# Instance normalisation over 512 images: row statistics by one reduce and one Square in place of sixteen BN_STATS, with fixed engine order and whole tiles at the end

## The chip, the cores and the metric

One core of one Trainium2 chip. The metric is the device time of one execution in microseconds (us); where several runs exist the median is quoted. Before: 1258.53 us (13 runs, 1258.19 to 1258.94).

A ratio between two kernels is the mean time of one kernel's fast runs over that of the other's of the same rounds. So it isn't quite the ratio of the medians quoted here. Now and then a single run came out too long, of the kernel before as well (1264.60 and 1267.03 us). Such runs still count as fast runs and widen the intervals, so I compare medians and traces and give the interval beside them where it matters. What makes those runs long I don't know.

## The reference

```python
# x: float32 [8, 64, 32, 64, 64]; eps = 1e-5
mean = np.mean(x, axis=(2, 3, 4), keepdims=True)
var = np.var(x, axis=(2, 3, 4), keepdims=True)
return ((x - mean) / np.sqrt(var + eps)).astype(np.float32)
```

That is 512 independent images of 131,072 values. The kernel has to read 268.44 MB and write 268.44 MB, and does little arithmetic on them.

## The kernel before

Eight images make a tile of 128 partitions x 8192 values (4 MiB), 16 partitions for one image. There are 64 tiles and six buffers. A tile is loaded, its statistics are taken, a matmul with a block-diagonal matrix of ones adds up the 16 partitions of each image, a chain of five tiny operations makes a scale and a bias of the sums, and one ScalarE pass normalises the tile in place, after which it is stored.

```python
for g in range(n_groups):                       # 64 tiles
    tail = g >= n_groups - 2
    lsplit = 4 if tail else LOAD_SPLIT          # LOAD_SPLIT = NSPLIT = 1
    nsplit = 4 if tail else NSPLIT
    x_tile = xpool.tile([P, F], FP32)           # six buffers, F = 8192
    ...
    for j in range(lsplit):                     # load, by columns
        nc.sync.dma_start(out=xv3[:, j, :], in_=xg3[:, j, :])

    stats6 = spool.tile([P, NCHUNK, 6], FP32)
    for c in range(NCHUNK):                     # 16 pieces of 512
        nc.vector.bn_stats(out=stats6[:, c, :], in_=xv[:, c, :])
    mv = spool.tile([P, 2], FP32)
    nc.vector.bn_aggr(out=mv[:], in_=stats6[:])
    # ... one tiny VectorE op, the matmul into psum_t, then ACT, DVE, ACT, DVE, DVE
    #     on one column each, giving sb = (scale, bias) ...
    for h in range(nsplit):
        nc.scalar.activation(out=yv[:, h, :], in_=yv[:, h, :], func=AF.Identity,
                             bias=sb[:, 1:2], scale=sb[:, 0:1])
        nc.gpsimd.dma_start(out=og[:, h, :], in_=yv[:, h, :])     # store
```

The order of the instructions on each engine is the scheduler's. The last two tiles ("the tail") are loaded, normalised and stored in four column pieces of 2048 values.

## Time and profile before

| | before |
|---|---|
| span in the profile | 1256.8 us |
| VectorE (DVE) busy, instructions | 55%, 1345 |
| ScalarE (ACT) busy | 39% |
| bytes, mean rate | 537.03 MB, 427 GB/s |
| instruction-fetch packets | 16 |
| last load lands, last store lands | 1232.1 us, 1253.1 us |

These lines of the page of the kernel before are its slice view (40 slices of 31.4 us; a digit is the busy share in tenths), its DMA queues (packets, MB, share of 16 engines' span) and two costly groups (busy us, mean ns | idle time of the engine before them and what ended it).

```profile
span 1256.8 us, 2298 instructions
DVE  5854645646556465464554645646556465464632
DMA  9999999999999999999999999999999999999996
GB/s 400 420 432 434 433 434 434 434 433 434 432 434 433 434 434 433 432 434 434 431 434 434 433 430 431 433 433 434 432 434 433 433 434 434 432 434 434 432 407 274
...
q1 hardware_dynamic: 10080, 268.44, 49.6%
q0 software_dynamic: 10080, 268.44, 49.6%
q14 instruction: 16, 0.13, 0.0%
...
L76 DVE BATCH_NORM_STATS2 stats<-x_tile 128x6 f32<-128x512 f32 x1024 | 614.9, 684 | 452.0 <-DMA x_tile<-in_x_dram 452.0
L128 ACT ACTIVATE x_tile<-x_tile,sb 128x8192 f32<-128x8192 f32 (+1 forms) x70 | 463.3, 6626 | 49.5 <-DVE sb L113 49.5
...
x_tile<-in_x_dram SPq DMA_DIRECT2D x62, 4096.0 KB, 48.4
out_dram<-x_tile POOLq DMA_DIRECT2D x62, 4096.0 KB, 48.6
```

The DMA row is full until the last slice; no engine row is. So in the middle of the kernel only the DMA counts. VectorE's 452 us of waiting for loads are not lost time but spare capacity. Apart from the start (400 and 420), the last two columns of the rate row (407 and 274) are the only place where the DMA falls off. The row `q14 instruction` counts the packets that fetch the engines' instructions, of all engines together.

The windows view of the same kernel cuts out that place. Its columns are the stretch in us, its length, busy us (and instructions) of PE, PEld, DVE, ACT and POOL, the granted clock, the DMA engines' mean busy share, and GB/s. A DMA packet counts in the stretch in which it starts, so a share can come out a little over 1.

```profile
1160.00:1200.00 40.00, 1.12 (x4) 1.00 (x4) 22.26 (x43) 8.14 (x5) 0.53 (x1) 1.00 1.00 431
1200.00:1214.00 14.00, 0.00 (x0) 0.00 (x0) 7.16 (x13) 7.21 (x1) 0.53 (x1) 1.00 1.00 421
1214.00:1224.00 10.00, 0.56 (x2) 0.50 (x2) 3.59 (x9) 0.47 (x2) 0.00 (x0) 1.00 0.98 421
1224.00:1232.00 8.00, 0.00 (x0) 0.00 (x0) 4.74 (x9) 3.90 (x2) 0.53 (x1) 1.00 0.17 70
1232.00:1245.00 13.00, 0.56 (x2) 0.50 (x2) 3.92 (x10) 12.19 (x9) 3.19 (x6) 1.00 0.99 403
```

From 1224 to 1232 us the DMA engines are 17% busy: most of them have nothing to do.

The DMA view of the kernel before, for 1165 to 1198 us alone, shows how the two queues share the engines while the loads of the tail are in flight (q0 is the stores, q1 the loads; packets, MB, share).

```profile
q0 software_dynamic: 368, 10.94, 76.8%
q1 hardware_dynamic: 363, 3.35, 23.9%
```

The packet counts are almost equal, the bytes are not: most load packets are 8 KB there (a quarter of a row), the stores' are 32 KB (a whole row).

One more reading comes from the trace itself. Each transfer counts sixteen completions, one from each DMA engine. This table, not part of the profile page, gives for some loads of the kernel before how long after the middle completion the last one came, and when the nearest instruction-fetch packets started.

```
load landed at     126   145 | 165   262 | 282   379 | 399   496 | 516    1158 us
last minus middle  1.3   1.3 | 2.1   1.9 | 2.8   2.5 | 3.2   3.0 | 3.8     7.3 us
fetch packet at          149.7       266.5       383.4       500.3  us
```

Each of these packets is followed by a step of 0.7 to 0.9 us, and little of it is made up before the next. Not every fetch packet is: the one at 239.8 us, for instance, left the last completion where it was (2.0 us at 223 and at 243 us).

### The profile page before, as it was taken

The numbers are of one execution on the slowest core, as the hardware profiler recorded it, in microseconds if no ns is written. First come the engines' busy times: TensorE is split into PE (matmuls) and PEld (weight loads), VectorE is DVE, ScalarE is ACT, GpSimd is POOL, SyncE is SP. The second block draws the span as 40 slices with busy tenths as digits, with TensorE's granted clock in tenths as the row PEclk, the third lists the DMA queues.
The fourth block names the chain that finished last, engine by engine and source line by source line (L and its number), as shares of the span: only waits on it lengthen the run. The fifth ranks groups of instructions, "written<-read, shape, count | busy, mean of one in ns | idle before, by whom it ended". The sixth has DMA issues, their size and how long they took to land.

```text
span 1256.8 us, 2298 instructions
## 1 busy us (share of the span) xinstructions
PE 35.9 (3%) x128; PEld 32.0 (3%) x128; DVE 695.7 (55%) x1345; ACT 495.9 (39%) x201; POOL 38.2 (3%) x76
## 2 busy tenths in 40 slices
PE   0000000000000000000000000000000000000000
PEld 0000000000000000000000000000000000000000
DVE  5854645646556465464554645646556465464632
ACT  2544243342443434424334243342443434424225
POOL 0000000000000000000000000000000000000001
DMA  9999999999999999999999999999999999999996
GB/s 400 420 432 434 433 434 434 434 433 434 432 434 433 434 434 433 432 434 434 431 434 434 433 430 431 433 433 434 432 434 433 433 434 434 432 434 434 432 407 274
DMA packets 20177, 537.03 MB, mean 427 GB/s; under 512 B 2240, under 2 KB 2240, under 8 KB 2240
## 3 DMA queue, kind: packets, MB, share of 16 engines
q1 hardware_dynamic: 10080, 268.44, 49.6%
q0 software_dynamic: 10080, 268.44, 49.6%
q14 instruction: 16, 0.13, 0.0%
q8 instruction: 1, 0.02, 0.0%
HBM read 268.44 MB, written 268.44 MB: 427 GB/s over the span
## 4 chain that ended last, share of the span: by engine, by line
issue 78%; DMA 14%; DVE 3%; POOL 2%; ACT 2%; PE 0%; POOLq 0%; ACTq 0%; SPq 0%
DMA x_tile<-in_x_dram 9%; DMA out_dram<-x_tile 6%; POOL out_dram L135 2%; DVE stats L76 2%; ACT x_tile L128 2%; DVE mv L78 0%; PE psum_t L90 0%; POOLq L135 0%; ACT tmp L104 0%; DVE mv L80 0%; POOLq L169 0%; ACT tmp L95 0%; DVE sb L112 0%; DVE sb L113 0%; DVE tmp L96 0%
## 5 line engine op out<-in xcount | busy, mean ns | idle before, releaser
L76 DVE BATCH_NORM_STATS2 stats<-x_tile 128x6 f32<-128x512 f32 x1024 | 614.9, 684 | 452.0 <-DMA x_tile<-in_x_dram 452.0
L128 ACT ACTIVATE x_tile<-x_tile,sb 128x8192 f32<-128x8192 f32 (+1 forms) x70 | 463.3, 6626 | 49.5 <-DVE sb L113 49.5
L95 ACT ACTIVATE tmp<-psum_t 128x1 f32<-128x1 f32 x64 | 11.0, 171 | 684.9 <-PE psum_t L90 684.8
L135 POOL DMA_DIRECT2D out_dram<-x_tile x70 | 37.4, 534 | 1205.7 <-ACT x_tile L128 1204.3
L90 PE MATMUL psum_t<-mv,block_ones 128*128 128x2 f32 x128 | 35.9, 350 | 1200.3 <-DVE mv L80 1200.3
L90 PEld LDWEIGHTS psum_t<-mv,block_ones 128*128 128x128 f32 x128 | 32.0, 310 | 1204.1 <-issue 1094.8
L96 DVE SCALAR_TENSOR_TENSOR tmp<-psum_t,tmp 128x1 f32<-128x1 f32 x64 | 10.1, 158 | 58.7 <-ACT tmp L95 58.7
L78 DVE BATCH_NORM_AGGREGATE mv<-stats 128x2 f32<-128x96 f32 x64 | 37.6, 588 | 2.1
L104 ACT ACTIVATE tmp<-tmp,eps_tile 128x1 f32<-128x1 f32 x64 | 18.8, 294 | 14.2 <-DVE tmp L96 14.2
L112 DVE RECIPROCAL sb<-tmp 128x1 f32<-128x1 f32 x64 | 10.5, 163 | 23.5 <-ACT tmp L104 23.5
L80 DVE SCALAR_TENSOR_TENSOR mv<-mv 128x1 f32<-128x1 f32 x64 | 14.0, 219 | 2.2
L113 DVE SCALAR_TENSOR_TENSOR sb<-psum_t,sb 128x1 f32<-128x1 f32 x64 | 10.1, 158 | 2.1
masks.py:370 ACT ACT_TABLE_LOAD x1 | 1.3, 1283 | 0.8 <-PEq L155 0.8
L104 ACT ACT_TABLE_LOAD x1 | 1.3, 1283 | 0.0
L55 DVE MEMSET eps_tile<- 128x1 f32 x1 | 0.1, 59 | 0.9 <-PEq L155 0.9
masks.py:371 POOL TENSOR_SCALAR_AFFINE_SELECT block_ones<-block_ones 128x128 f32<-128x128 f32 x1 | 0.3, 332 | 2.0 <-ACT block_ones masks.py:370 2.0
masks.py:383 POOL TENSOR_SCALAR_AFFINE_SELECT block_ones<-block_ones 128x128 f32<-128x128 f32 x1 | 0.3, 344 | 0.1
masks.py:370 ACT ACTIVATE block_ones<-block_ones 128x128 uint32<-128x128 uint32 x1 | 0.3, 309 | 0.0
L155 POOL MEMSET const-float32-0.0<- 128x1 f32 x1 | 0.1, 98 | 0.3 <-issue 0.3
L155 POOL MEMSET const-bfloat16-1.0<- 128x1 bf16 x1 | 0.1, 101 | 0.0
L155 POOL MEMSET const-uint8-127<- 128x1 uint8 x1 | 0.1, 101 | 0.0
L155 POOL MEMSET const-float32-1.0<- 128x1 f32 x1 | 0.1, 98 | 0.0
## 6 DMA issues: line engine op xcount, KB each, us to landing
x_tile<-in_x_dram SPq DMA_DIRECT2D x62, 4096.0 KB, 48.4
out_dram<-x_tile POOLq DMA_DIRECT2D x62, 4096.0 KB, 48.6
x_tile<-in_x_dram SPq DMA_DIRECT2D x8, 1024.0 KB, 56.5
out_dram<-x_tile POOLq DMA_DIRECT2D x8, 1024.0 KB, 6.0
```

The costliest lines, as they stand in the source:

```text
L76: nc.vector.bn_stats(out=stats6[:, c, :], in_=xv[:, c, :])
L78: nc.vector.bn_aggr(out=mv[:], in_=stats6[:])
L80: nc.vector.scalar_tensor_tensor(out=mv[:, 1:2], in0=mv[:, 0:1], scalar=mv[:, 0:1], in1=mv[:, 1:2], op0=ALU.mult, op1=ALU.add,)
L90: nc.tensor.matmul(psum_t[:], lhsT=block_ones[:], rhs=mv[:], start=True, stop=True)
L95: nc.scalar.activation(out=tmp[:, 0:1], in_=psum_t[:, 0:1], func=AF.Square)
L96: nc.vector.scalar_tensor_tensor(out=tmp[:, 1:2], in0=psum_t[:, 1:2], scalar=float(PPI), in1=tmp[:, 0:1], op0=ALU.mult, op1=ALU.subtract,)
L104: nc.scalar.activation(out=tmp[:, 2:3], in_=tmp[:, 1:2], func=AF.Sqrt, bias=eps_tile[:, 0:1], scale=1.0 / (PPI * PPI),)
L112: nc.vector.reciprocal(out=sb[:, 0:1], in_=tmp[:, 2:3])
L113: nc.vector.scalar_tensor_tensor(out=sb[:, 1:2], in0=psum_t[:, 0:1], scalar=-1.0 / PPI, in1=sb[:, 0:1], op0=ALU.mult, op1=ALU.mult,)
L128: nc.scalar.activation(out=yv[:, h, :], in_=yv[:, h, :], func=AF.Identity, bias=sb[:, 1:2], scale=sb[:, 0:1],)
L135: nc.gpsimd.dma_start(out=og[:, h, :], in_=yv[:, h, :],)
L155: nc = _bacc.Bacc("TRN2", target_bir_lowering=False, num_devices=1)
```

## The change

The intent: fewer and cheaper VectorE instructions for the statistics. The sum comes from one reduce over the whole row on VectorE, the sum of squares from one Square with an accumulator on ScalarE at the same time, whose element output goes to a scratch tile of 8-bit floats. The program order on these two engines is fixed, and the cut of the last two tiles is dropped.

```diff
-    for g in range(n_groups):
-        lsplit = 4 if tail else LOAD_SPLIT
-        nsplit = 4 if tail else NSPLIT
+    junk = cpool.tile([P, F], mybir.dt.float8e4)
+    with tc.manual_schedule(engines={mybir.EngineType.DVE, mybir.EngineType.Activation}):
+        for g in range(n_groups):
+            lsplit = LOAD_SPLIT
+            nsplit = NSPLIT
 ...
-        for c in range(NCHUNK):
-            nc.vector.bn_stats(out=stats6[:, c, :], in_=xv[:, c, :])
-        nc.vector.bn_aggr(out=mv[:], in_=stats6[:])
-        nc.vector.scalar_tensor_tensor(...)        # mean^2 + var
+            nc.vector.reduce_sum(out=s[:, 0:1], in_=x_tile[:], axis=AX.X)
+            nc.scalar.activation(
+                out=junk[:], in_=x_tile[:], func=AF.Square,
+                accum_out=s[:, 1:2], saturate=False,
+            )
 ...   # matmul and the small chain as before, with other constants; then normalise and store
```

## The prediction

> **What bounds it now.** The DMA engines: the slice view shows them 90% busy or more in 39 of 40 slices, at 430 to 434 GB/s; 537.03 MB at 434 GB/s is 1237 of the 1256.8 us span. VectorE is 55% busy, ScalarE 39%. A tile's cycle through the six buffers is some 116 us: load 48.4 us from issue to landing, store 48.6, and only about 20 from landing to store issue. So faster statistics in the middle shorten nothing.
>
> **Costs.** Per tile the change removes sixteen BN_STATS (9.59 us in a row), BN_AGGREGATE (0.59) and one small operation (0.22). It adds a reduce over 8192 elements on VectorE and, beside it, a Square with accumulator on ScalarE. The Trainium skill, "VectorE: DVE Perf Modes", section "The perf-mode tier table", gives tensor_reduce its slowest mode only; no trace here shows one yet. Estimate from BN_STATS (599 ns per 512): 8.6 to 8.8 us. Square: the same-size Identity took 7.21, so 7.1 to 7.4. Landing to store issue falls from 20 to 18 us. ScalarE rises to 15 us of the 19.4 us period: no bottleneck.
>
> **Where I expect a gain: two places, seen at the end.**
> 1. Of the sixteen completion counts of each load, the last comes ever later than the middle one: 1.3 us at 126 us, 7.3 at 1158. It grows in steps of about 0.75 us at 8 KB instruction-fetch packets (149.7, 266.5, 383.4, 500.3, 617.1 us...), one per six tiles, when VectorE has run some 128 instructions. (The Trainium skill, "Runtime: NRT & Kernel Launch", "Instruction fetch mechanics": a sequencer fetches its instructions by DMA.) So VectorE's fetches delay one DMA engine, and each transfer ends with its slowest. VectorE goes from 21 instructions a tile to 4, some 9 fetches become about 2, and 5 us of lag go.
> 2. The tail is cut in four: its loads travel in 8 KB packets against the stores' 32 KB and get a quarter of their rate (80 against 330 GB/s, 1164 to 1200 us). The last lands at 1232.1. Stores run dry meanwhile (ScalarE's pass over tile 61 waits 9.7 us behind a BN_STATS of the next tile), and DMA share is 0.17 in 1224 to 1232. Whole-tile loads should land by 1212, and the last store be issued near 1230, while older stores still occupy the DMA.
>
> At 1164 us the trace still has 9.9 MB of loads and 25 MB of stores to move. At 434 GB/s mixed (46 us), then 420 to 432 store-only (15 MB, 35 to 36 us), that ends at about 1245, plus 1 to 3 us of remaining lag: 1247, against 1253.1 now. The last 3.7 us of span and 1.7 to the measured time stay.
>
> **Prediction: 1252.3 us** (0.5% less), 8 in 10 between 1249 and 1256.8. Faster by over 2%: 0.01; within 2%: 0.96; slower by over 2%: 0.03.
>
> **Right if:** the DMA row stays at 9 to the last slice; fetch packets drop from 16 to 7 or fewer; the lag at 1150 us is under 3 us; VectorE under 50%, ScalarE near 75%; reduce about 8.7 us.
>
> **Wrong if:** the lag is no matter of fetches (then 1256 to 1258); the stores run dry before the last, leaving a bare 18 us chain (1258 to 1262); Square's 8-bit output or accumulator takes twice as long, so that ScalarE passes 19 us a tile (much slower); or mixed traffic slows.

## The result, and the profile after

1250.34 us (9 runs, 1250.24 to 1250.45) against 1258.53 us. The ratio is 0.9935, 95% interval 0.9925 to 0.9944: 8.2 us less, a small difference but clear of the noise, and inside the predicted range.

The same lines of the page of the kernel after (here a slice is 31.2 us):

```profile
span 1248.6 us, 1262 instructions
DVE  5554534535445354453544535435345354453541
DMA  9999999999999999999999999999999999999998
GB/s 403 420 437 437 434 429 432 436 437 431 426 437 436 436 431 427 437 435 436 431 429 436 435 435 431 429 434 437 434 429 431 436 436 434 428 433 436 437 433 345
...
q14 instruction: 8, 0.06, 0.0%
...
L77 DVE TENSOR_REDUCE s<-x_tile 128x1 f32<-128x8192 f32 x64 | 555.9, 8685 | 516.4 <-DMA x_tile<-in_x_dram 516.4
L78 ACT ACTIVATE junk<-x_tile 128x8192 fp8e4<-128x8192 f32 x64 | 449.8, 7028 | 99.3 <-DMA x_tile<-in_x_dram 99.3
...
L78 ACT ACTIVATION_READ_ACCUMULATOR junk<-x_tile 128x1 f32 x64 | 11.9, 186 | 0.0
...
x_tile<-in_x_dram SPq DMA_DIRECT2D x64, 4096.0 KB, 50.8
out_dram<-x_tile POOLq DMA_DIRECT2D x64, 4096.0 KB, 47.3
```

The middle is the same as before: the trace moves 433.2 GB/s between 600 and 1150 us in both kernels. ScalarE is now 76% busy and VectorE 47%, which changes nothing. The fetch packets fell from 16 to 8; one of the 8 started 0.1 us into the span, and in the other traces it came just before the span, so like for like it is 16 against 7. The windows view of the kernel after for the same stretches:

```profile
1200.00:1214.00 14.00, 0.56 (x2) 0.50 (x2) 3.77 (x5) 9.41 (x6) 0.53 (x1) 1.00 1.04 447
1214.00:1224.00 10.00, 0.56 (x2) 0.50 (x2) 7.59 (x4) 7.00 (x5) 0.00 (x0) 1.00 0.97 419
1224.00:1232.00 8.00, 0.00 (x0) 0.00 (x0) 0.00 (x0) 6.23 (x1) 0.53 (x1) 1.00 1.05 455
1232.00:1245.00 13.00, 0.00 (x0) 0.00 (x0) 0.00 (x0) 0.00 (x0) 0.00 (x0) 1.00 0.78 338
```

The hole at 1224 to 1232 us is gone (share 0.17 to 1.05), and the DMA works until it has nothing left (0.78 in 1232 to 1245 us, in which the engines finish). The last load lands at 1212.4 us (1232.1 before), the last store is issued at 1230.5 us and lands at 1245.1 us (1253.1 before). In the DMA view for 1165 to 1198 us of the kernel after, equal packets now carry equal bytes:

```profile
q0 software_dynamic: 248, 7.34, 51.5%
q1 hardware_dynamic: 251, 7.18, 50.4%
```

Last minus middle completion of the loads near 1155 us: 1.9 us (7.3 before).

### The profile page after: what moved, and what is told of

Read it like the earlier page. It is cut to its first block, busy times and chain, and to the rows that moved or that the text cites. A ratio compares the mean times of both kernels' runs of the same rounds, so it can differ in the third digit from the quotient of the medians.

```text
span 1248.6 us, 1262 instructions
## 1 busy us (share of the span) xinstructions
PE 35.9 (3%) x128; PEld 32.1 (3%) x128; DVE 586.2 (47%) x257; ACT 949.3 (76%) x323; POOL 35.0 (3%) x70
## 4 chain that ended last, share of the span: by engine, by line
issue 51%; DVE 18%; another core or an unknown queue 16%; ACT 10%; PE 1%; POOL 1%; DMA 1%; POOLq 0%; ACTq 0%
DVE s L77 17%; ACT x_tile L120 5%; ACT junk L78 4%; PE psum_t L84 1%; POOL out_dram L127 1%; DMA x_tile<-in_x_dram 1%; ACT tmp L100 1%; ACT tmp L89 0%; DVE sb L104 0%; DVE tmp L92 0%; DVE sb L105 0%; ACT L100 0%; POOLq L161 0%; POOLq L127 0%
## 5 line engine op out<-in xcount | busy, mean ns | idle before, releaser
L77 DVE TENSOR_REDUCE s<-x_tile 128x1 f32<-128x8192 f32 x64 | 555.9, 8685 | 516.4 <-DMA x_tile<-in_x_dram 516.4
L78 ACT ACTIVATE junk<-x_tile 128x8192 fp8e4<-128x8192 f32 x64 | 449.8, 7028 | 99.3 <-DMA x_tile<-in_x_dram 99.3
L120 ACT ACTIVATE x_tile<-x_tile,sb 128x8192 f32<-128x8192 f32 x64 | 461.6, 7212 | 30.4 <-DVE sb L105 30.4
L84 PE MATMUL psum_t<-s,block_ones 128*128 128x2 f32 x128 | 35.9, 350 | 1185.9 <-DVE s L77 1076.4
L127 POOL DMA_DIRECT2D out_dram<-x_tile x64 | 34.1, 534 | 1193.7 <-ACT x_tile L120 1193.7
L84 PEld LDWEIGHTS psum_t<-s,block_ones 128*128 128x128 f32 x128 | 32.1, 311 | 1189.6 <-issue 1079.5
L78 ACT ACTIVATION_READ_ACCUMULATOR junk<-x_tile 128x1 f32 x64 | 11.9, 186 | 0.0
```

Of the source, the lines that this page charges most:

```text
L77: nc.vector.reduce_sum(out=s[:, 0:1], in_=x_tile[:], axis=AX.X)
L78: nc.scalar.activation(out=junk[:], in_=x_tile[:], func=AF.Square, accum_out=s[:, 1:2], saturate=False,)
L84: nc.tensor.matmul(psum_t[:], lhsT=block_ones[:], rhs=s[:], start=True, stop=True)
L127: nc.gpsimd.dma_start(out=og[:, h, :], in_=yv[:, h, :],)
```

## The experiments

**Theory.** The DMA is the bound everywhere, and the gain is two things: VectorE's instruction fetches delay one DMA engine, whose lag every transfer waits for (about 5.4 us, the difference of the lags), and the tail was cut in a way that starved its loads (about 2.8 us, the rest).
**Rival A:** the tail alone is the whole gain. **Rival B:** the shorter statistics, or the fixed order, are the gain. **Rival C:** the lag is no matter of fetches; sixteen BN_STATS reading SBUF disturb the DMA.

All runs gave correct results. The tables give medians; the kernel before ran in the same rounds at 1258.39 to 1258.61 us.

### e1: the kernel before, tail whole

```diff
-        lsplit = 4 if tail else LOAD_SPLIT
-        nsplit = 4 if tail else NSPLIT
+        lsplit = LOAD_SPLIT
+        nsplit = NSPLIT
```

> The kernel before with the last two tiles loaded and stored whole, nothing else changed. Two-part theory (instruction-fetch lag of one DMA engine, about 5.4 us, plus the cut tail, about 2.8 us): only the tail part comes, about 1255.7 us; last load lands near 1218 us, and the last completion count of a load at 1150 us still lags the middle one by about 7.3 us. Rival A (the tail alone is the whole gain): 1250.3 us. Rival B (the shorter statistics or the order of the engines' programs are the gain): 1258.5 us.

1256.51 us (six runs, four of them 1255.92 to 1256.60, the others 1258.91 and 1262.63), 1.9 us under the kernel before. Because of the two long runs the interval of the ratio, 0.9981 to 1.0009, isn't clear of 1; e9 below repeats it more cleanly. The trace agrees with the theory: the last load landed at 1216.7 us, the lag stayed at 7.3 us, and this line of the windows view shows the hole of 1224 to 1232 us filled (0.17 before).

```profile
1224.00:1232.00 8.00, 0.56 (x2) 0.50 (x2) 3.58 (x9) 3.39 (x3) 0.00 (x0) 1.00 0.97 418
```

Rival A falls: with the hole gone and the lag still there, the tail by itself is worth about a quarter of the gain.

### e9: the kernel after with the statistics of the kernel before

```diff
-            nc.vector.reduce_sum(...)
-            nc.scalar.activation(..., func=AF.Square, accum_out=...)
+            for c in range(NCHUNK):
+                nc.vector.bn_stats(...)
+            nc.vector.bn_aggr(...)
+            # and the small chain of the kernel before; the scratch tile, now unused, is left out
```

> The kernel after (whole tail, program order on VectorE and ScalarE) with the statistics of the kernel before (16 BN_STATS and a BN_AGGREGATE). Theory: the program order is worth nothing, so as e1: 1255.5 to 1256.5 us, lag at 1150 us 7.3 us. Rival B1 (the order is part of the gain): clearly under e1. Rival B2 (the shorter statistics chain is the gain, not the fetches): over 1257 us.

1256.10 us (1255.95 to 1256.33), ratio to the kernel before 0.9975 (0.9958 to 0.9992), lag 7.7 us, 16 fetch packets. Whole tail and fixed order together save 2.4 us, about the same as the whole tail without the fixed order (e1). The remaining 5.8 us to the kernel after come with the new form of the statistics. What in it saves them, e2 and e3 say.

### e2 and e3: the kernel after with VectorE instructions that do nothing

```diff
+            for _ in range(17):            # 34 in e3
+                nc.vector.engine_nop()
             y_tile = x_tile
```

Seventeen a tile make it 21 VectorE instructions again, the number of the kernel before. They read and write nothing.

> The kernel after with 17 engine no-operations a tile added to VectorE's program, which touch no data and fit in its idle time: 21 instructions a tile as in the kernel before. Two-part theory: instruction-fetch packets rise from 8 to about 16, the lag at 1150 us from 1.9 to about 7.3 us, the time by about 5.4 us to 1255.7 us. Rivals A and B, and rival C (the lag comes from BN_STATS reading SBUF against the DMA, not from fetches): no change, 1250.3 us and a lag of 1.9 us.

> The same with 34 no-operations a tile. Two-part theory: about 17 more fetches than the kernel after, at about 0.75 us each on the same DMA engine, so a lag of 12 to 14 us at 1150 us and a time of 1260 to 1263 us. Rivals A, B and C: 1250.3 us.

| | after | e2 | e3 | before |
|---|---|---|---|---|
| VectorE instructions a tile | 4 | 21 | 38 | 21 |
| fetch packets | 8 (7 like for like) | 16 | 24 | 16 |
| last minus middle completion, load near 1160 us | 1.9 us | 7.3 us | 13.7 us | 7.3 us |
| time | 1250.34 us | 1256.10 us | 1262.64 us | 1258.53 us |

The first line here is from the page of the kernel after, the next two are from e2's, and the last is from e3's. They show that the engines of e2 worked as in the kernel after, and only the fetches differ (the no-operations do not count as busy):

```profile
PE 35.9 (3%) x128; PEld 32.1 (3%) x128; DVE 586.2 (47%) x257; ACT 949.3 (76%) x323; POOL 35.0 (3%) x70
...
PE 35.9 (3%) x128; PEld 32.1 (3%) x128; DVE 586.6 (47%) x257; ACT 949.3 (76%) x323; POOL 35.0 (3%) x70
...
q14 instruction: 16, 0.13, 0.0%
...
q14 instruction: 24, 0.20, 0.0%
```

Like for like, nine more packets cost 5.8 us and seventeen more cost 12.3 us: 0.6 to 0.7 us a packet. The completions of e2 tie the lag to the packets directly: it rises by 0.75 to 0.82 us at each of nine fetches some 117 us apart (161.5 to 1096.6 us) and does not rise between them. A packet itself moves 8 KB and took 0.31 us in the trace; why it delays its DMA engine by more than that stays open. No data moved and no engine worked more, so rival C falls, and rival B as an explanation of these 5.8 us. This is the strongest result: the new statistics are faster here because they are fewer instructions to fetch, not because they are less work.

### e4: the same no-operations on GpSimd

```diff
-    with tc.manual_schedule(engines={DVE, Activation}):
+    with tc.manual_schedule(engines={DVE, Activation, Pool}):
 ...
+            for _ in range(17):
+                nc.gpsimd.engine_nop()
```

> The kernel after with 17 no-operations a tile on GpSimd in place of VectorE (GpSimd too in program order). If a fetch costs time whichever engine it is for and lands on the same or another single DMA engine: about 8 to 9 more fetch packets, lag at 1150 us 5 to 8 us, time 1254 to 1257 us. If only VectorE's fetches cost, or the cost is VectorE's waiting and no fetch: 1250.3 us.

1252.94 us (1252.61 to 1253.15), 16 fetch packets, lag 4.6 us. With nine more packets like for like it is 2.6 us slower than the kernel after, less than the 5.8 us of e2 and under the expected range. The completions show why this number can't be read as the price of the nine packets. At the load near 1157 us the second-last completion is 3.2 us behind the middle one and the last 4.6 us. The second-last rises in steps of 0.45 to 0.54 us, each at one of six added fetches (440.7 to 1101.3 us). The last one has no step at any of them; it creeps up, from some 260 us on, by mostly 0.04 to 0.1 us from load to load, with a single step of 0.65 us near a fetch at 741.6 us, which the kernel after has too. At the end the two were level: they finished the last store at 1247.82 and 1247.83 us (1245.1 us in the kernel after). So fetches for GpSimd do delay a DMA engine, by less than those for VectorE, and by enough for the 2.6 us; but the lag of 4.6 us is mostly this creep, whose cause no run shows. That fetches of different engines go to different DMA engines fits, but the trace names no DMA engine, so it stays an inference. That GpSimd's order was fixed too was not tested alone.

### e5: the kernel after with the tail cut as before

```diff
-            lsplit = LOAD_SPLIT
-            nsplit = NSPLIT
+            lsplit = 4 if tail else LOAD_SPLIT
+            nsplit = 4 if tail else NSPLIT
```

> The kernel after with the loads and stores of the last two tiles cut in four again, as before the change. Two-part theory: loses only the tail part, about 1253 us; loads fall to about 80 GB/s in 1165 to 1195 us, the last load lands 10 to 20 us later than 1212 us. Rival A (the tail is the whole gain): 1258.5 us. Rival B: 1250.3 us.

1263.69 us (ratio to before 1.0043, 1.0031 to 1.0055): neither theory. The cut costs the kernel after 13.4 us, where it cost the kernel before about 2. The timeline of e5 (start, length, engine, line, operation, and in brackets the idle time before it and what ended it) shows why.

```profile
1191.66 0.53 POOL L127 DMA_DIRECT2D out_dram<-x_tile  x1 [18.87 <-ACT x_tile L120]
1216.16 7.03 ACT L78 ACTIVATE junk<-x_tile 128x8192 fp8e4<-128x8192 f32 x1 [24.79 <-DMA x_tile<-in_x_dram]
1216.17 8.69 DVE L77 TENSOR_REDUCE s<-x_tile 128x1 f32<-128x8192 f32 x1 [32.10 <-DMA x_tile<-in_x_dram]
1226.69 8.69 DVE L77 TENSOR_REDUCE s<-x_tile 128x1 f32<-128x8192 f32 x1
1226.76 8.05 ACT L120 ACTIVATE x_tile<-x_tile,sb 128x2048 f32<-128x2048 f32 x4 [0.47 <-DVE sb L105]
1234.72 7.02 ACT L78 ACTIVATE junk<-x_tile 128x8192 fp8e4<-128x8192 f32 x1
1243.67 8.05 ACT L120 ACTIVATE x_tile<-x_tile,sb 128x2048 f32<-128x2048 f32 x4 [0.47 <-DVE sb L105]
```

The loads are starved as in the kernel before, and no statistics can start until the fourth piece has landed (1216 us). Sixteen BN_STATS can follow the pieces as they come; one reduce over the row can't. Then ScalarE has to do Square and normalise for both tiles in turn, with little left for the DMA (share 0.26 in 1224 to 1232 us). So the tail's cut and the form of the statistics belong together: uncutting was no small tidying but a condition for the new statistics.

### e6, e7: only the loads cut, only the stores cut

```diff
-            lsplit = LOAD_SPLIT                 # e6
+            lsplit = 4 if tail else LOAD_SPLIT
-            nsplit = NSPLIT                     # e7
+            nsplit = 4 if tail else NSPLIT
```

> The kernel after with only the loads of its last two tiles cut in four by columns (8 KB pieces of a row). Theory: the 8 KB load packets are starved by the stores' 32 KB packets, so the loads come late; whole-tile statistics then leave a bare chain at the end, and whole stores make it longer than in e5: last load near 1226 us, time 1266 to 1268 us. Rival (the cut of the stores did the harm in e5): 1250.3 us.

> The kernel after with only the stores of its last two tiles cut in four. Theory: no harm, since the DMA queue is never empty then: 1249.8 to 1251 us. Rival (the cut of the stores did the harm in e5): over 1258 us.

e6 1266.89 us, e7 1250.84 us. The cut of the loads does all the harm, as expected; that of the stores changes 0.5 us. The DMA view of e6 for 1175 to 1208 us:

```profile
q0 software_dynamic: 399, 11.50, 80.7%
q1 hardware_dynamic: 399, 2.91, 20.9%
```

399 packets each: the DMA engines take one packet of each queue in turn, and a queue's share is the size of its packets. The Trainium skill, "DMA: Bandwidth & Descriptors", section "Queues, rings and completion order", says that each engine goes round-robin between its queues packet by packet; these counts agree, if the packets of the record are the page's (it describes them as groups of several descriptors). The rates are 88 GB/s for loads (2.91 MB in 33 us) against 348 GB/s for stores.

### e10: four loads by partitions, a test that was not clean

```diff
+                for j in range(4):         # the last two tiles
+                    nc.sync.dma_start(out=x_tile[32*j : 32*j+32, :], in_=xr[32*j : 32*j+32, :])
```

> The kernel after with the loads of its last two tiles cut in four by partitions: four loads of 1 MB each as in e6, but every packet 32 KB as in a whole load. If the size of the packets starves the loads: no starvation, last load near 1212 us, 1250 to 1251 us. If the number of loads, or the order in which they are issued, does the harm: as e6, over 1260 us.

1262.73 us, where I had expected 1250 to 1251. The packets were 32 KB and took turns as meant, but the DMA became slower. The DMA view of e10 for 1178 to 1220 us:

```profile
DMA packets 629, 15.60 MB, mean 371 GB/s; under 512 B 153, under 2 KB 153, under 8 KB 153
...
q0 software_dynamic: 313, 8.78, 51.0%
q1 hardware_dynamic: 316, 6.82, 49.0%
```

371 GB/s in place of 433, with load packets of 1.58 us on average in place of 1.21. While loads into 32 partitions ran, the whole DMA was slower. The Trainium skill, "SBUF — State Buffer", section "Door 1: The DMA port swizzle", says that partitions 0 to 31 reach eight of the sixteen ports; the slower packets agree with it in direction. So e10 changed two things at once and decides nothing about packet size; e11 was made for that.

### e11: cut tail, but the stores that compete with it cut too

```diff
-            lsplit = LOAD_SPLIT
-            nsplit = NSPLIT
+            lsplit = 4 if tail else LOAD_SPLIT
+            nsplit = 4 if g >= n_groups - 8 else NSPLIT
```

> As e5 (the kernel after, last two tiles loaded and stored in four pieces), but the stores of the last eight tiles are cut in four too, so that the small load packets meet store packets of the same 8 KB. If the DMA engines take one packet of each queue in turn and the size of the packets is what starved the loads: loads keep about 215 GB/s in 1165 to 1198 us (84 in e5), the last load lands near 1213 us, and the time returns to 1250 to 1252 us. If the number of loads or of issues did the harm: about 1263 us, as e5.

1254.01 us (1253.62 to 1254.46), 9.7 us faster than e5 with the same loads. The DMA view of e11 for 1165 to 1198 us:

```profile
q0 software_dynamic: 966, 7.06, 51.0%
q1 hardware_dynamic: 964, 6.98, 50.1%
```

The loads are back at 212 GB/s (102 in e5 over the same stretch; the 84 of the expectation holds only from about 1174 us, when all its load packets are small). So packet size was the cause, not the number of loads. The last load landed near 1203 us, 10 us earlier than I had expected, because the same thing happened the other way round before: from 1120 to 1150 us whole loads in 32 KB packets met stores in 8 KB packets, and the loads had about 350 GB/s against 80. That head start helps e11's time, so it is the rates that show the cause, more than the time. The time missed my range by 2 us: with 8 KB packets the stores alone ran at 424 GB/s from 1204 to 1244 us (433 with 32 KB packets in the kernel after, 1211 to 1242 us), and the span ended 4.8 us after the last packet instead of 3.9 us. Small packets are a little slower even when nothing competes; why the end took longer I did not look into.

### e8: the kernel after in the scheduler's own order

```diff
-    with tc.manual_schedule(engines={DVE, Activation}):
+    if True:
```

> The kernel after without the fixed program order on VectorE and ScalarE, as the scheduler orders them by itself. Theory: off the critical path in the middle, so within 1 us of 1250.3 us unless the last stores are held back at the end (then up to 10 us more, and the profile shows the last store issued later than 1231 us). Rival B1 (the order is part of the gain in the middle): over 1253 us with the last store issued as before.

1265.32 us (1262.05 to 1268.87), 15 us slower, the harm being at the end and not in the middle: the last load landed at 1212.2 us, as in the kernel after (1212.4). The timeline of e8:

```profile
1212.20 8.69 DVE L77 TENSOR_REDUCE s<-x_tile 128x1 f32<-128x8192 f32 x1 [10.42 <-DMA x_tile<-in_x_dram]
1221.19 7.21 ACT L120 ACTIVATE x_tile<-x_tile,sb 128x8192 f32<-128x8192 f32 x1 [1.80 <-DVE sb L105]
1228.69 0.53 POOL L127 DMA_DIRECT2D out_dram<-x_tile  x1 [18.84 <-ACT tmp L89]
1229.07 14.30 ACT L120 ACTIVATE x_tile<-x_tile,sb 128x8192 f32<-128x8192 f32 x2
1236.57 0.53 POOL L127 DMA_DIRECT2D out_dram<-x_tile  x1 [7.34 <-ACT x_tile L120]
1243.67 0.53 POOL L127 DMA_DIRECT2D out_dram<-x_tile  x1 [6.57 <-ACT x_tile L120]
```

The scheduler's order puts a later tile's Square in front of an earlier tile's normalising. Sixteen microseconds after the last load has landed, three stores are still to be issued. In the windows view of e8 the DMA share falls to 0.44 (188 GB/s) in 1224 to 1232 us. A tile waited some 66 us for its store in the middle (tile 50 landed at 946.9 us, its store was issued at 1013.1 us), and that cost nothing there.

### e12: the small operations of two tiles together

```diff
+    steps = [[0], [1]] + [[g, g + 1] for g in range(2, n_groups - 4, 2)] + ...   # last four single
+    # K = 2: two reduces and Squares, then one matmul on [P, 4]
+    # and each of the five small operations on two columns
```

> The kernel after with the small operations of two tiles done together (single tiles at both ends): about 5 VectorE and 8 ScalarE instructions for two tiles in place of 8 and 12, one matmul in place of two. A tile then waits some 19 us longer for its store, which the theory says is free in the middle. Fetch theory: 1 to 3 fewer instruction fetches, lag at 1150 us down from 1.9 to 1.0 to 1.6 us, 1249.3 to 1250.2 us. If the time from landing to store issue mattered in the middle: slower than 1251 us.

1250.17 us median (five runs 1250.03 to 1250.92, one 1260.67), 6 fetch packets and a lag of 1.7 us (just over the expected 1.0 to 1.6). One packet fewer, like for like, was too few to show in the time: the spans are 1248.6 us both. It is no better version, but a sharp control against rival B: the first tile of a pair waits some 37 us for its store (tile 50 landed at 960.4 us, store issued at 997.9 us) and the last load lands at 1212.4 us all the same.

## Why the prediction was right

- **The bound.** Right. The DMA row stays at 9 up to the last slice, which has 8. 433.2 GB/s in the middle of both kernels; e8 and e12 lengthen a tile's wait for its store by tens of us and make no landing in the middle later (tile 50 landed at 960.4 us in the kernel after and in e12, at 946.9 us in e8).
- **Durations.** Right: the reduce took 8.69 us (estimate 8.6 to 8.8), the Square 7.03 us and 0.19 us for its accumulator (7.1 to 7.4), landing to store issue 18.1 us (18), ScalarE 76% busy. The Trainium skill, "VectorE: DVE Perf Modes", section "The perf-mode tier table", has tensor_reduce at its slowest mode; 8685 ns for 8192 elements agrees: my estimate for one element a cycle at that page's clock of 0.96 GHz is 8533 ns, 152 ns less than measured.
- **Fetch lag.** Right, and shown by e2 and e3: the packets fell from 16 to 8, or 7 like for like ("7 or fewer"), the lag from 7.3 to 1.9 us, worth 5.8 us. The Trainium skill, "Runtime: NRT & Kernel Launch", section "Instruction fetch mechanics", says that a sequencer fetches its instructions by its own DMA queue; that agrees with the fetch queue q14 of the profile. It calls the cost of a block boundary mostly hidden; in a kernel bound by DMA it wasn't.
- **Tail.** Right in its mechanism: starvation by packet size (e6, e11), and a DMA that never runs dry at the end. (Its 80 GB/s for the loads hold from 1178 to 1200 us; over all of 1164 to 1200 us, with the end of a whole tile in it, the trace has 104.) The 9.7 us wait of ScalarE's pass over tile 61 was not tested alone; in e1 it is gone with the cut (tile 61 landed at 1178.0 us, its store was issued at 1197.9 us). The last load landed at 1212.4 us (1212) and the last store was issued at 1230.5 us (near 1230). What the cut cost was 1.9 to 2.4 us in the frame of the kernel before (e1, e9). I had not seen that it would have cost 13.4 us in the frame of the new one (e5), nor that the fixed order is worth 15 us there (e8). Neither was needed for the number, because the change did both things at once.
- **The size.** 1252.3 us predicted, 1250.34 us measured. The term of the sum that was mis-sized is "then 420 to 432 store-only (15 MB, 35 to 36 us)". The trace has 14.1 MB of stores left when the middle DMA engine finishes its loads (1210.4 us), not 15, and the stores alone ran at 433 GB/s with 32 KB packets, not at the lower rate that I took partly from the 8 KB packets of the old tail. The middle engine finished at 1243.1 us, after 32.7 us in place of 35 to 36. That is the 2 us; the other terms came out as predicted (loads done at 1210, remaining lag 2.0 us).

## What to carry to other kernels

When the DMA queues are full from start to end, look for gains only where they are not full, or where one of the sixteen engines is behind the others: the spread of a transfer's completions shows it. In this kernel each 128 VectorE instructions cost some 0.7 us of the critical DMA engine, so fewer, larger instructions paid even though VectorE had time to spare. Cut the last tiles only if the pieces move in packets as large as those they compete with, and only if the work on a piece can start before the rest has landed. Even that is no promise: in no run here did cutting the tail pay (2 us lost in the kernel before, 13.4 in e5, 16.5 in e6, 0.5 in e7, and 3.7 in e11, where the packets were equal).

## What the Trainium skill lacked or had wrong

- "Runtime: NRT & Kernel Launch", "Instruction fetch mechanics": it says that fetching is mostly hidden. Here fetch packets of 8 KB (the page has blocks of 16 KiB), one per about 128 VectorE instructions, each cost one DMA engine about 0.7 us: 9 packets more, 5.8 us (e2); 17 more, 12.3 us (e3). For GpSimd the steps were 0.45 to 0.54 us (e4). No page gives what fetches cost the kernel's own transfers.
- "DMA: Bandwidth & Descriptors", "Queues, rings and completion order": it has the turn by packets, but not the consequence that a queue's share follows the size of its packets: 88 against 348 GB/s for loads of 8 KB and stores of 32 KB (e6), 212 against 214 with 8 KB both (e11), about 350 against 80 for loads of 32 KB and stores of 8 KB (e11, 1120 to 1150 us).
- "SBUF — State Buffer", "Door 1: The DMA port swizzle": it gives rates for one narrow transfer. It lacks what narrow loads do beside full-width stores: 371 GB/s in all instead of 433, load packets of 1.58 us instead of 1.21 (e10).
- "ScalarE: Activation LUTs" mentions an accumulator output but not its cost: a separate read of 186 ns after each Square. The Square with its 8-bit output took 7028 ns, the Identity pass with a 32-bit output 7212 ns; a Square with a 32-bit output was not run, so no effect of the output's type is shown.
